# Memory queries and memory outputs on scaled float16 pairs in a hybrid attention block on Trainium2

## The chip, the cores and the metric

The kernel runs on one core of one Trainium2 chip. Its time is the device time of one execution in microseconds (us). Times before and after are medians of a few executions; a profile is one further execution, with every instruction recorded. The engines are named as in the profile: PE multiplies matrices (PEld is its loading of weights), DVE is the vector engine, ACT the scalar engine, POOL is GpSimd, and SP issues nearly all DMAs.

## What is computed

One layer on x (1024 rows of 1024), with a memory of 256 rows; each sub-layer stands between two RMS norms, and its output is added to x. Cut to what matters:

```
def memory_cross_attention(h, mem_n, w_mq, w_mk, w_mv, w_mo):
    q = (h @ w_mq).reshape(B, S, MEM_HEADS, MEM_HEAD_DIM)      # 4 heads of 256
    k = (mem_n @ w_mk).reshape(B, M, MEM_HEADS, MEM_HEAD_DIM)
    v = (mem_n @ w_mv).reshape(B, M, MEM_HEADS, MEM_HEAD_DIM)
    logits = einsum('bshd,bmhd->bhsm', q, k) * (MEM_HEAD_DIM ** -0.5)
    p = softmax(logits)
    o = einsum('bhsm,bmhd->bshd', p, v).reshape(B, S, D_MODEL)
    return o @ w_mo

    h = rmsnorm(x, g_mix_pre);  proj = h @ w_in
    y = [forgetting attention (8 heads), chunked attention (8 heads)], each normed, concatenated
    x = x + rmsnorm(y @ w_out, g_mix_post)
    h = rmsnorm(x, g_mem_pre);  mem_n = rmsnorm(mem, g_mem_kv)
    x = x + rmsnorm(memory_cross_attention(h, mem_n, ...), g_mem_post)
    h = rmsnorm(x, g_ff_pre)
    x = x + rmsnorm(square(relu(h @ w_ff1)) @ w_ff2, g_ff_post)
```

All inputs and the output are float32.

## The kernel before

**Products from pairs.** Every large product is computed from two parts of each operand, a high part (the value rounded to a narrower type) and a low part (what is left), by three matmuls: high by high, high by low, low by high (`mm3`, lines 203 to 206). The parts are fp32r, a four-byte form of float32, or float16. Before the change the q, k and v projections of the attention and the whole MLP use float16 pairs; float16 has a small range of exponents, so there the weights are first brought to a known size by a power of two that is computed from their squares. The memory keys and values, the output projection `w_out`, the memory queries (`mq`) and the memory output (`ym`) use fp32r pairs without scales.

**Stages.** The opening computes the norm of x and the first values, written out by hand in order, up to about 58 us of the profile. Then comes the attention phase: projections of eight pairs of heads, scores, softmax, turning of the probabilities and products with the values, and, as filler, the memory's keys and values. The second phase holds the output projection (`yw`, with matmuls from 511 us), the rows with their norms (`close_row`), the turning of the rows (`tr_h2T`), the queries, the memory attention and its output. The queries of all 1024 rows and the output of the first 512 rows are computed with seven products in place of eight quarter products (a Strassen scheme, `QUERIES` and `PRODUCTS`), for which sums and differences of weight blocks and of operands are made beforehand (`QuerySums`, `Sums`, `Forms`, `operand_parts`). The other 512 rows of the output are plain (`product_steps` and the rows at the end). The MLP follows from about 830 us to the end.

**What sets the order.** Between the opening and the MLP no order is written by hand. The class `Flow` is a planner that runs while the program is built. It keeps a time of its own; a stream of PE steps gives for each step a cost and a condition, and at each point the first stream whose step is ready is taken. Work of the other engines is handed to `flow.put(engine, earliest time, cost, call, what follows, level)`: of the waiting items that could start, the one with the lowest level is emitted next. The engines on the chip then run their own instructions in the order emitted, and semaphores make them wait for data. So a wrong cost in the plan does not make the result wrong, but it puts an instruction in a queue ahead of others that could have run. `flow.free` holds the times at which each engine is free at the start; `BUSY` sets them after the opening (DVE 8.0, ACT 5.0, POOL 5.5). Tiles are counted by tokens in `free`: a step waits until the plan has one.

**The weights.** `Stock` loads each block of 128 x 1024 float32 (line 459), has ACT make the high part (`hi`, line 508; for q, k and v line 498) and DVE, or for some mk blocks POOL in two halves, the low part (`lo`, lines 514 and 518). Three raw tiles are in flight at most. `needs` says which tiles a block takes.

**Lines that the prediction touches.** Line 471 computes the squares of a q, k or v block on ACT, line 481 sums them on PE (`nq`), line 493 scales a block on POOL. Lines 2254 to 2256 are the last conversions of the opening: for each of eight pieces of the second half of x, ACT makes the high part and DVE (POOL for pieces 6 and 7) the low part, emitted one after the other ahead of the planned phase. Line 338 is a cast of value weights on POOL in the opening. Lines 745 to 747 are the softmax scaling on POOL, line 1746 the same in the memory attention. Line 1190 (`square_sum`) is the square of a row on ACT, lines 1422 and 1423 the root of the row's mean square on DVE and POOL, line 1434 the scaled row on ACT. Lines 1226 to 1241 load blocks of `w_mo`, take their differences and store them; lines 1360 to 1374 do so for `w_mq`. Lines 1633 and 1635 split the operands of the queries; line 1741 finds a score row's maximum.

## Time and profile before

| | us |
|---|---|
| median of 3 executions (lowest, highest) | 1422.49 (1420.89, 1424.1) |
| the profiled execution | 1422.69 |
| its span, first to last instruction | 1420.7 |

| stage, us | PE busy | DVE busy | ACT busy | POOL busy |
|---|---|---|---|---|
| 0 to 58, opening | 53.96 | 43.44 | 37.98 | 12.27 |
| 440 to 520, last heads, memory keys and values | 79.74 | 65.25 | 67.00 | 37.64 |
| 520 to 607, output projection, rows | 85.35 | 54.91 | 55.99 | 9.86 |
| 830 to 1421, MLP | 577.17 | 510.77 | 377.41 | 67.76 |

Busy time is the time in which an engine executes at least one instruction. Matmuls overlap: each is shown longer than the distance to the next, so a row of the timeline gives its start, its duration, engine, line, operation, the tile written and the tiles read, and the distance of two starts is what a matmul costs. A row of a group gives the line, engine, operation, names, shapes, count, busy time and mean duration, and after the second bar the idle time of the engine just ahead of it with what ended it. A row of the waits gives who waited for whom, the total, the number of times and the longest. The granted clock of PE is 0.999 over the span.

### The profile page before, as it was taken

The page shows a single profiled execution, that of the slowest core. Times are in us where ns is not written, and L with a number is a line of the kernel's source. Part 1 is how long each engine was busy: PE and PEld are TensorE (multiplying, and loading weights), DVE is VectorE, ACT ScalarE, POOL GpSimd, SP SyncE. Part 2 cuts the span into 40 slices and gives each one's busy share as a digit, 9 for nine tenths or more (in the row PEclk, how much of TensorE's full clock was granted, in tenths as well). Part 3 has the DMA queues.
Part 4 walks back from the last instruction along what each step waited for, and adds up shares of the span by engine and source line. Part 5 has one row for each costly group of instructions (what it writes and reads, how often), then busy time and mean ns, then how long its engine had stood idle before and what let it go on. Part 6 is the DMA issues. An engine that isn't in the chain of part 4 may idle for free.

```text
span 1420.7 us, 22525 instructions
## 1 busy us (share of the span) xinstructions
PE 1394.8 (98%) x7681; PEld 917.3 (65%) x7681; DVE 1152.9 (81%) x1863; ACT 987.1 (69%) x1688; POOL 452.6 (32%) x615
## 2 busy tenths in 40 slices
PE   8999999999999999999999999999999999999998
PEld 8746666666668988787888864444444445666653
DVE  7887787877768865779788878677998887899998
ACT  6667888888778855897466545786677757666654
POOL 2367868887646500221102421003233000000003
PEclk9999999999999999999999999999999999999999
DMA  8132465545526578472234546976888998696885
GB/s 284 49 83 81 130 196 171 170 131 170 146 84 183 176 249 302 171 266 83 75 104 147 193 160 245 338 235 234 290 285 284 362 364 296 233 318 219 313 297 208
DMA packets 118802, 295.72 MB, mean 208 GB/s; under 512 B 13448, under 2 KB 31888, under 8 KB 118688
## 3 DMA queue, kind: packets, MB, share of 16 engines
q1 hardware_dynamic: 118544, 294.03, 61.4%
q8 instruction: 60, 0.98, 0.3%
q14 instruction: 54, 0.44, 0.1%
q10 hardware_dynamic: 144, 0.26, 0.1%
HBM read 220.26 MB, written 65.59 MB: 201 GB/s over the span
## 4 chain that ended last, share of the span: by engine, by line
PE 75%; DVE 10%; ACT 6%; issue 5%; DMA 2%; POOL 1%; SPq 0%; DVEq 0%; ACTq 0%; POOLq 0%
PE ptr L804 4%; PE fx L204 3%; PE fx L206 3%; PE fx L205 3%; PE px L206 2%; PE px L204 2%; PE px L205 2%; PE pv L849 2%; PE yw L204 2%; PE yw L205 2%; PE yw L206 2%; PE mq L205 2%; PE mq L206 2%; PE mq L204 2%; PE k L204 2%
## 5 line engine op out<-in xcount | busy, mean ns | idle before, releaser
L814 ACT ACTIVATE phl<-ptr 128x512 f16<-128x512 f32 (+3 forms) x152 | 79.5, 537 | 25.5 <-PE ptr L804 22.7
L2900 POOL TENSOR_SCALAR rf<-sf 128x1 f32<-128x1 f32 x7 | 5.8, 826 | 280.3 <-ACT jf L2879 280.0
L2595 POOL TENSOR_TENSOR sc<-wf,wf 128x512 f32<-128x512 f32 x8 | 11.2, 1396 | 172.4 <-DMA wf<-in_w_ff 122.8
L810 DVE SCALAR_TENSOR_TENSOR phl<-ptr,phl 128x384 f16<-128x384 f32 (+1 forms) x76 | 45.8, 616 | 14.5 <-ACT phl L814 14.1
L1746 POOL TENSOR_SCALAR mp<-mp,mst 128x256 f32<-128x256 f32 x32 | 21.3, 673 | 108.8 <-DVE mst L1745 102.1
L812 DVE TENSOR_TENSOR phl<-ptr,phl 128x384 fp32r<-128x384 f32 (+1 forms) x76 | 46.6, 617 | 8.5 <-ACT phl L814 7.8
L2744 ACT ACTIVATE vhif<-ra,fsc 128x1024 f16<-128x1024 f32 x34 | 38.9, 1144 | 21.1 <-PE fx L206 10.2
L849 PE MATMUL pv<-phl,vs 128*128 128x512 f32 (+1 forms) x152 | 52.8, 428 | 0.0
L2746 DVE SCALAR_TENSOR_TENSOR vhif<-ra,fsc,vhif 128x1024 f16<-128x1024 f32 x34 | 43.5, 1281 | 10.6 <-ACT vhif L2744 10.3
L2744 ACT ACTIVATE whif<-ra,fsc 128x1024 f16<-128x1024 f32 x34 | 38.9, 1143 | 18.8 <-PE fx L206 10.3
L204 PE MATMUL yw<-whiwo,yT_hi 128*128 128x512 f32 x128 | 50.8, 397 | 0.0
L205 PE MATMUL yw<-wlowo,yT_hi 128*128 128x512 f32 x128 | 50.2, 392 | 0.0
L206 PE MATMUL yw<-whiwo,yT_lo 128*128 128x512 f32 x128 | 50.1, 391 | 0.0
L204 PE MATMUL fx<-vlof,vhif 128*128 128x512 f16 x128 | 48.5, 379 | 0.8 <-DVE yc L2951 0.8
L204 PE MATMUL q<-hF_hi,wq 128*128 128x512 f16 x128 | 48.9, 382 | 0.2 <-DVE qs L953 0.2
L204 PE MATMUL k<-hF_hi,wk 128*128 128x512 f16 x128 | 49.0, 383 | 0.0
L2746 DVE SCALAR_TENSOR_TENSOR whif<-ra,fsc,whif 128x1024 f16<-128x1024 f32 x34 | 43.5, 1280 | 6.5 <-ACT whif L2744 6.4
L206 PE MATMUL q<-hF_hi,wq 128*128 128x512 f16 x128 | 48.5, 379 | 0.0
L204 PE MATMUL fx<-wlof,whif 128*128 128x512 f16 x128 | 48.5, 379 | 0.0
L205 PE MATMUL fx<-wlof,whif 128*128 128x512 f16 x128 | 48.5, 379 | 0.0
L206 PE MATMUL fx<-wlof,whif 128*128 128x512 f16 x128 | 48.5, 379 | 0.0
L205 PE MATMUL k<-hF_lo,wk 128*128 128x512 f16 x128 | 48.5, 379 | 0.0
(855 smaller groups left out, 5338.5 us busy)
## 6 DMA issues: line engine op xcount, KB each, us to landing
wg<-in_w_ff SPq DMA_DIRECT2D x48, 512.0 KB, 5.7
ra<-gd SPq DMA_DIRECT2D x40, 512.0 KB, 5.3
wf<-in_w_ff SPq DMA_DIRECT2D x38, 512.0 KB, 4.8
wn<-in_w_ff SPq DMA_DIRECT2D x32, 512.0 KB, 4.9
w2n<-in_w_ff SPq DMA_DIRECT2D x32, 512.0 KB, 6.0
wi<-in_w_ff2q SPq DMA_DIRECT2D x28, 512.0 KB, 5.5
gd<-s SPq DMA_DIRECT2D x32, 256.0 KB, 5.6
gd<-g SPq DMA_DIRECT2D x19, 256.0 KB, 5.0
```

The lines of the kernel that those rows point to most:

```text
L204: nc.tensor.matmul(ps, lh, rh, start=start, stop=False, skip_group_check=more)
L205: nc.tensor.matmul(ps, lh, rl, start=False, stop=False, skip_group_check=more)
L206: nc.tensor.matmul(ps, ll, rh, start=False, stop=stop, skip_group_check=more)
L804: nc.tensor.transpose(tr[:, m, :], sp[:, k * P:(k + 1) * P], ident)
L810: flow.put("V", at, 0.75, lambda: nc.vector.scalar_tensor_tensor(pl[:, live, :], tr[:, live, :], 2.0 ** 14, ph[:, live, :], op0=ALU.mult, ...
L812: if ph.dtype == F16 else nc.vector.tensor_sub(pl[:, live, :], tr[:, live, :], f(ph[:, live, :])), done)
L814: flow.put("S", flow.end, 0.6, lambda ph=ph, tr=tr, live=live: nc.scalar.activation(ph[:, live, :], tr[:, live, :], AF.Copy, scale=2.0 ** ...
L849: nc.tensor.matmul(pv[:, :, qs_, :], v, hl[:, :, hs, :], start=c == 0 and turn == 0, stop=last)
L1746: mul = lambda st=st, pr=pr: nc.gpsimd.tensor_scalar(pr, pr, st[:, 2:3], 1.0, op0=ALU.mult, op1=ALU.mult)
L2595: eng.tensor_sub(sc[:, k1], r0[:, k0], r1[:, k0])
L2744: nc.scalar.activation(ah, ra, AF.Copy, scale=su)
L2746: nc.vector.scalar_tensor_tensor(al, ra, su, ah, op0=ALU.mult, op1=ALU.subtract)
```

## The change

**Pairs.** The blocks of `w_mq` and `w_mo` and the operands that meet them (the forms of the queries, the operands of the Strassen products, the outputs of the second half) become float16 pairs. One tile holds high and low part, so each takes half as many buffers.

**Scales.** Two numbers per side bring the operands to size. For the queries: the squares of all blocks of `w_mq` (16 new squares on ACT, in `QuerySums`) and of `g_mem_pre` are summed by one small matmul, and from them come powers of two `smq` (weights) and `sgm` (multiplied into `g_mem_pre`), and `uq`, which takes both out again and holds the factor 0.0625. For the output: the squares of all blocks of `w_mo` (16, in `Sums`) and of the memory values (2) give `smo` and `sov`; `sov` goes into the scaling of the memory probabilities on POOL, and `um` (into `g_mem_post`) and `um32` (into the squares) take both out. New streams `query_scale_steps` and `output_scale_steps` hold the two matmuls. The conversion of a `mq` block waits for the query scales, that of a `mo` block and every memory score for the output scales.

**High parts on POOL.** All blocks mk, mv, wo, mq and mo get their high part from POOL in place of ACT. The scaled rows 1, 3, 5 and 7 move from ACT to POOL.

**The opening.** The eight pieces of lines 2254 to 2256 are handed to the planner; `BUSY` becomes DVE 5.6, ACT 4.5, POOL 7.4, and the plan holds the first k weights and the squares of the second q block as done at 5.9 and 0.5.

**Order.** Nearly all levels given to `flow.put` change, some streams change places, the costs in the plan follow the new types (0.681 to 0.655 for three query matmuls, 1.362 to 1.31 for six of the output), some small tiles get more buffers, and the starts and distances of background loads change.

```
+    fsm, mfx = const.tile([P, 42], F32, name="fsm"), const.tile([P, 8], F32, name="mfx")
+    gmem, gmsq = (const.tile([P, KC], F32, name=k) for k in ("gmem", "gmsq"))
...
+            if key[0] in ("mq", "mo"):
+                shape.insert(1, 2)
+                x = (u4(nm, shape, F16) if home == "u4" else
+                     (p2x if home == "wq" else wp).tile(shape, F16, tag=home, bufs=2, name=nm))
+                self.w[key] = x[:, 0], x[:, 1]
+                c = smq if key[0] == "mq" else smo
+                if eng == "G":
+                    return nc.gpsimd.tensor_scalar(x[:, 0], raw, c, 1.0, op0=ALU.mult, op1=ALU.mult)
+                return nc.scalar.activation(x[:, 0], raw, AF.Copy, scale=c)
...
-            nc.scalar.activation(w[0], raw, AF.Copy)
+            if eng == "G":
+                nc.gpsimd.tensor_copy(w[0], raw)
+            else:
+                nc.scalar.activation(w[0], raw, AF.Copy)
...
+            if key[0] in ("mq", "mo"):
+                return eng.scalar_tensor_tensor(lo, raw, smq if key[0] == "mq" else smo, hi, op0=ALU.mult, op1=ALU.subtract)
...
-                if not free[home].ready(n):
+                if not free[home].ready(n) or not there(*{"mq": ("query scales",), "mo": ("output scales",)}.get(key[0], ())):
...
-                flow.put("S", flow.now, 1.06, lambda key=key: self.hi(key), halves, 2)
+                e = {"mk": "G", "mv": "G", "wo": "G", "mq": "G", "mo": "G"}[key[0]]
+                flow.put(e, flow.now, 1.06 if e == "S" else 1.15, lambda key=key, e=e: self.hi(key, e), halves, 3)
...
-        START, PACE = 100.0, 12.0
+        START, PACE = 20.0, 14.0
...
+            landed = all_of(("sum blocks", i, a), 4, lambda at: [flow.put("S", at, 0.65, lambda k=k, c=24 + i * 8 + a * 4 + m: square_sum(
+                r[k], fsm[:, c:c + 1], HT, 1.0), squared, 5) for m, k in enumerate(names4)])
...
-            form_q[n] = [u4(f"{n}q_{m}{i}", (P, 2, HT)) for m in "hl" for i in range(2)]
+            both = [u4(f"{n}q{i}", (P, 2, 2, HT), F16) for i in range(2)]
+            form_q[n] = [both[i][:, m] for m in range(2) for i in range(2)]
...
-                    yield (0.72, lambda: there(("qm", th, h, 0), ("qm", th, h, 1)) and free["s"].ready()
+                    yield (0.72, lambda: there(("qm", th, h, 0), ("qm", th, h, 1), "output scales") and free["s"].ready()
...
-                        pr, pr, st[:, 2:3], 1.0, op0=ALU.mult, op1=ALU.mult)
+                        pr, pr, st[:, 2:3], sov, op0=ALU.mult, op1=ALU.mult)
...
-            opt[n, k] = u4(f"{n}o{k}", (P, 2, 2, Q))
+            opt[n, k] = u4(f"{n}o{k}", (P, 2, 2, Q), F16)
...
-                            outs[th, h] = u4(f"oT_hi{th}{h}", (P, 2, HT)), u4(f"oT_lo{th}{h}", (P, 2, HT))
+                            x = u4(f"oT{th}{h}", (P, 2, 2, HT), F16)
+                            outs[th, h] = x[:, 0], x[:, 1]
...
-        yield 0.87, lambda: flow.now > GATES and free["tr"].ready(2)
+        yield 0.87, lambda: flow.now > GATES and there(*(("hF", kc) for kc in range(KC))) and free["tr"].ready(2)
...
+    def late_half(kc, x):
+        eng = "G" if kc in LATE else "V"
+        hi = lambda: nc.scalar.activation(hF[1].hi(kc), x, AF.Copy)
+        lo = lambda: (nc.gpsimd if eng == "G" else nc.vector).tensor_sub(hF[1].lo(kc), x, hF[1].hi(kc))
+        flow.put("S", 0.0, 0.63, hi, lambda at: flow.put(
+            eng, at, 1.45 if eng == "G" else 1.15, lo, mark(("hF", kc)), 1), 3)
+
-    LATE, RAWS, GATES, BUSY = (6, 7), (0.0, 3.5), 5.0, dict(V=8.0, S=5.0, G=5.5)
+    LATE, RAWS, GATES, BUSY = (6, 7), (0.0, 3.5), 5.0, dict(V=5.6, S=4.5, G=7.4)
...
         for kc in range(KC):
-            x, e = xT[1][kc // 2][:, kc % 2, :], nc.gpsimd if kc in LATE else nc.vector
-            nc.scalar.activation(hF[1].hi(kc), x, AF.Copy)
-            e.tensor_sub(hF[1].lo(kc), x, hF[1].hi(kc))
+            late_half(kc, xT[1][kc // 2][:, kc % 2, :])
+        seen["k", 0], seen["sq", ("q", 1)] = 5.9, 0.5
...
+        for m in range(2):
+            flow.put("S", 0.0, 1.25, lambda m=m: square_sum(f(vmh[m]), fsm[:, 40 + m:41 + m], D, 1.0), mark(("vm squares", m)), 0)
...
-        flow.run([memory_out_steps(), memory_turn_steps(), memory_score_steps(), rstd_steps(1), second_rows(),
-                  norm_steps(), tail], lambda: stock.to_load or stock.to_split)
+        flow.run([memory_turn_steps(), rstd_steps(1), memory_score_steps(), memory_out_steps(), second_rows(),
+                  norm_steps(), output_scale_steps(), tail], lambda: stock.to_load or stock.to_split)
```

More of the change, by code (lines that the diff above doesn't have):

```diff
@@ L565, in pump @@
                 if key[0] in "qkv":
[L566 removed]
+                    flow.put("S", flow.now, 1.25, lambda key=key: self.squares(key), mark(("sq", key)), 5)
                     continue
@@ L867, in both @@
                             o2[own], pv[own, :, ::step], uv[own], o2[own], op0=ALU.mult, op1=ALU.add), lambda end: (
-                            free["pv"].give(end), store(end)))
+                            free["pv"].give(end), store(end)), 1)
                     flow.put("S", flow.end, 0.45, lambda: nc.scalar.activation(
-                        o2[own], pv[oth, :, ::step], AF.Copy, scale=uv[oth]), both)
+                        o2[own], pv[oth, :, ::step], AF.Copy, scale=uv[oth]), both, 3)
                     return
@@ L966, in then @@
                         flow.put("V", at, 0.75, lo, lambda end: (last(end), flow.load(
-                            end, lambda: copy(l), part, 3.6)), 1)
-                    flow.put("S", flow.end, 0.7, hi, then, 1)
+                            end, lambda: copy(l), part, 3.6)), 5)
+                    flow.put("S", flow.end, 0.7, hi, then, 2)
         if 1 in halves:
@@ L1272, in squares @@
                     nc.vector.tensor_reduce(wsq[:, n:n + 1], r[0], axis=mybir.AxisListType.X, op=ALU.max)
-            flow.load(flow.now, load, lambda at: flow.put("S", at, 1.25, squares, lambda end: (free["u4"].give(end), seen.__setitem__(("wn", n), end)), 5))
+            flow.load(flow.now, load, lambda at: flow.put("S", at, 1.25, squares, lambda end: (free["u4"].give(end), seen.__setitem__(("wn", n), end)), 3))
     def rsqrt(x, k):
@@ L1350, in pump @@
                 _, call, then = self.parts.pop(0)
-                flow.put("V", flow.now, 0.7, call, then, 5)
+                flow.put("V", flow.now, 0.7, call, then, 2)
                 self.at = flow.now + self.PACE
@@ L1355, in unit, with squares @@
             r = {}
-            landed = all_of(("query sums", nb), 4)
+            squared = all_of(("query sums", nb), 4)
+            def squares(at):
+                for m, k in enumerate(("B11", "B12", "B22", "B21")):
+                    flow.put("S", at, 0.65, lambda k=k, c=nb * 4 + m: nc.scalar.activation(
+                        self.junk, r[k], AF.Square, accum_out=fsm[:, c:c + 1]), squared, 5)
+            landed = all_of(("query blocks", nb), 4, squares)
             for k, (kh, nh) in {"B11": (0, 0), "B12": (0, 1), "B22": (1, 1), "B21": (1, 0)}.items():
@@ L1443, in wait @@
             else:
-                flow.put("G", end + 0.5, 0.0, lambda: None, wait)
-        flow.put("G", at, 1.9, lambda: root(0, ss[:, 0:1], ss[:, 1:2]), wait, 0)
+                flow.put("G", end + 0.5, 0.0, lambda: None, wait, 1)
+        flow.put("G", at, 1.9, lambda: root(0, ss[:, 0:1], ss[:, 1:2]), wait, 5)
     def mix_steps(g):
@@ L1697, in query_steps @@
             if i:
-                for _ in range(4):
+                for _ in range(2):
                     free["u4"].give(flow.end)
```

217 lines of the change are left out of this document (130 added, 87 removed).

## The prediction

> **What bounds the kernel now.** I read the page first, then the busy time by stages, then the waits of PE, and last single rows of the timeline.
>
> ```profile
> span 1420.7 us, 22525 instructions
> ...
> PE 1394.8 (98%) x7681; PEld 917.3 (65%) x7681; DVE 1152.9 (81%) x1863; ACT 987.1 (69%) x1688; POOL 452.6 (32%) x615
> ```
>
> The page gives PE busy in 1394.8 of 1420.7 us, so PE is idle for 25.9 us in all. The profiled execution took 1422.69 us; 2.0 us of it lie around the span. The median of the three runs, 1422.49, is 0.2 us lower, and I shift the sum by that at its end.
>
> With PE at 98%, only two things make the program shorter: matmuls that follow each other faster, or less idle PE. The stages (columns: us, then PE, PEld, DVE, ACT and POOL busy) show where the change could do either:
>
> ```profile
> 58.00:100.00 42.00, 37.73 (x184) 17.15 (x182) 34.58 (x50) 31.01 (x50) 27.70 (x28) 1.00 0.32 91
> 100.00:440.00 340.00, 339.63 (x2006) 227.77 (x2005) 258.76 (x617) 274.90 (x556) 244.64 (x387) 1.00 0.48 144
> ...
> 607.00:830.00 223.00, 221.21 (x1121) 185.04 (x1120) 185.22 (x303) 142.85 (x277) 52.69 (x66) 1.00 0.44 145
> ```
>
> From 58 to 100 us, where the opening's conversions run, PE is idle for 42.00 - 37.73 = 4.3 us; in the attention stage that follows for 0.4 us. From 607 to 830 us, which holds the memory queries, attention and output, it is idle for 1.8 us, and DVE is busy in 185 of 223 us, ACT in 143. There the pace of the matmuls sets the end, with DVE next. What ended PE's idle time, first in the opening (window 0 to 100), then around the memory stage (511 to 830):
>
> ```profile
> PE nq L481 <- ACT wk L471: 2.6, 2, 2.1
> ```
>
> ```profile
> PE tr_h2T L1555 <- ACT yw L1434: 1.6, 1, 1.6
> PE mq L205 <- DVE A12q_l L1635: 0.7, 1, 0.7
> PE mq L205 <- DVE A22q_l L1635: 0.6, 1, 0.6
> ```
>
> **Float16 pairs.** These rows of the tiles mq and ym give the counts:
>
> ```profile
> 0.00:1421.00 1421.00, 82.34 (x336) 1.00 0.62 208
> ```
>
> ```profile
> L204 PE MATMUL ym<-whimo,oT_hi x64: 389/389/476, 779.3 to 829.1; 128*128 128x512 f32 x64
> ...
> L204 PE MATMUL ym<-whimo_B,A11o x8: 389/396/437, 715.8 to 723.6; 128*128 128x512 f32 x8
> ```
>
> The queries are 336 matmuls. The outputs of the second half are three passes (L204 to L206) of 64, 192; those of the first half are seven products of three passes of 8, 168. That is 696 matmuls of 512 columns, all fp32r now, all float16 after. Durations overlap, so I take the distance between starts. First and last of 13 consecutive query matmuls, then of 18 output matmuls, then of 22 float16 ones in the first MLP product:
>
> ```profile
> 663.07 0.39 PE L206 MATMUL mq<-S2q_h,wlomq_T 128*128 128x512 f32 x1
> ...
> 665.79 0.39 PE L206 MATMUL mq<-S2q_h,wlomq_T 128*128 128x512 f32 x1
> ```
>
> ```profile
> 720.08 0.39 PE L204 MATMUL ym<-whimo_B,A11o 128*128 128x512 f32 x1
> ...
> 724.01 0.39 PE L206 MATMUL ym<-whimo_B,A11o 128*128 128x512 f32 x1
> ```
>
> ```profile
> 836.92 0.38 PE L205 MATMUL px<-h3T_lo,whi_a 128*128 128x512 f16 x1
> ...
> 841.45 0.38 PE L205 MATMUL py<-h3T_lo,whi_a 128*128 128x512 f16 x1
> ```
>
> 2.72 / 12 = 226.7 ns, 3.93 / 17 = 231.2 ns, 4.53 / 21 = 215.7 ns. The gain is 11.0 to 15.5 ns each; I take the middle, 13.2, since both fp32r rows are from this stage: 696 x 13.2 ns = 9.2 us, with bounds of 7.7 and 10.8. It lies on PE, which sets the end there, if DVE lets it.
>
> [...]
>
> **The high parts that go to GpSimd.** All conversions of the 60 weight blocks mk, mv, wo, mq and mo (line 508) leave ACT, and GpSimd gets them. The columns are ACT's busy time and count; then the nearest rows of GpSimd, a scaling of 1024 columns and a cast of 512:
>
> ```profile
> 0.00:1421.00 1421.00, 62.87 (x60) 1.00 0.62 208
> ```
>
> ```profile
> L493 POOL TENSOR_SCALAR wrawk<-wrawk,wsc 128x1024 f32<-128x1024 f32 x8 | 9.0, 1119 | 0.8 <-ACT wk L524 0.8
> ```
>
> ```profile
> L338 POOL CAST whiv<-wrawv 128x512 fp32r<-128x512 f32 x4 | 3.4, 868 | 9.1 <-DMA wrawv<-in_w_v 9.1
> ```
>
> Between 60 x 1.12 = 67 us and 60 x 2 x 0.87 = 104 us enter a GpSimd that is busy for 452.6 us in all and 52.7 of the 223 us. I take 1.12, the row with the right number of columns. The 36 query and output blocks (14, 14 and 8) put 40 us there: room enough. Behind a conversion in GpSimd's queue stand the softmax scalings (L1746, L747) and the row roots (L1423); PE's 1.6 us wait on ACT's yw is behind such a root. Ahead of ACT's rows stands a microsecond less for each block, and four of the eight row scalings of L1434 leave ACT too. The three waits around the memory stage sum to 2.9 us; the two on DVE stay, part of the first goes: a gain of 1.0, bounds +2 (roots later) and -2.9.
>
> The low part after such a conversion is computed by DVE from two SBUF operands. Three rows of DVE, 1024 columns each: the scaled form that the query and output blocks get now, the plain form in the memory stage, and the plain form of mk, most of which runs while GpSimd is busy for 16.5 of 20 us (GpSimd's time is the last of the five in the second fence):
>
> ```profile
> L2746 DVE SCALAR_TENSOR_TENSOR whif<-ra,fsc,whif 128x1024 f16<-128x1024 f32 x34 | 43.5, 1280 | 6.5 <-ACT whif L2744 6.4
> ...
> L514 DVE TENSOR_TENSOR wlomq_T<-wrawmq_T,whimq_T 128x1024 fp32r<-128x1024 f32 x8 | 9.7, 1218 | 0.0
> ...
> L514 DVE TENSOR_TENSOR wlomk<-wrawmk,whimk 128x1024 fp32r<-128x1024 f32 x4 | 5.9, 1487 | 0.7 <-ACT whimk L508 0.7
> ```
>
> ```profile
> 440.00:460.00 20.00, 19.74 (x163) 18.71 (x162) 17.12 (x37) 18.11 (x38) 16.53 (x21) 1.00 0.56 167
> ```
>
> The scaled form adds 62 ns x 36 = 2.2 us to DVE. A collision adds 269 ns; if each of the 36 conversions meets one, 9.7 us. With about 3 us of small scale arithmetic (some 15 operations of at most 0.2 us), DVE has 185.2 + 2.2 + 9.7 + 3 = 200 us of work in a stage of 223 - 9.2 = 214 us: not the bound, but with little to spare in its fullest stretches. I price it at a loss of 1.0, bounds 0 and 4.
>
> [...]
>
> **The scales.** 16 squares of query blocks and 16 of output blocks join ACT, and two of 1024 columns:
>
> ```profile
> L1190 ACT ACTIVATE junk<-yw 128x512 bf16<-128x512 f32 x16 | 10.1, 630 | 6.1 <-DVE yw L1474 5.9
> ```
>
> 32 x 0.63 and two of at most twice that are 23 us, most of them at the lowest rank of ACT's list, against the 62.87 us that leave it. Two small matmuls on PE cost at most one full step each, 2 x 0.23 = 0.5; I take 0.4, bounds 0 and 1. The new waits: no query block is converted before the query scales, no memory score starts before the output scales. In before the last difference block of the output weights is issued at 557.5 and the first score starts at 625.4:
>
> ```profile
> L1241 SPq DMA_DIRECT2D T4d<-B21r x4: 319/320/320, 528.6 to 557.5; - x4
> ```
>
> ```profile
> L204 PE MATMUL ms<-km_hi,qh x64: 277/280/370, 625.4 to 778.6; 128*128 128x256 f32 x64
> ```
>
> With 10 us allowed for landing, 10 us for 16 squares and 5 us for the root and its arithmetic (estimates; the squares from the row above), the scales are there near 583, some 40 us ahead of the score. What is queued behind that wait is the whole memory attention, but the wait ends first. The query sums start 80 us earlier than before, so theirs ends earlier still. Both at 0.
>
> **The opening.** Eight high and eight low parts go from a fixed place into the list, with the engines' real busy times as its start. In before they sit in one block, and the square that PE waits for stands behind the eight:
>
> ```profile
> 62.47 4.28 ACT L2255 ACTIVATE hF_hi<-xT 128x512 f16<-128x512 f32 x8
> ...
> 67.84 0.38 PE L481 MATMUL nq<-nq,o 128*128 128x1 f32 x2 [2.13 <-ACT wk L471]
> ```
>
> The norm matmul waits 2.13 us in PE's in-order queue with projections behind it that could run. A list that knows of the 4.28 us puts it later: a gain of 2.1. What is late next is DVE's or GpSimd's share of the first heads; bounds from all the idle of this stretch, -4.3, to a loss of 1. The changed ranks and the order of the streams elsewhere move no work: 0, with 2 either way, since PE is full from 100 to 440 us.
>
> **Sum.** -9.2 - 1.0 + 1.0 + 0.4 - 2.1 = -10.9: 1422.7 - 10.9 = 1411.8 for a profiled execution, 1411.6 as a median.
>
> **Rivals.** (1) DVE becomes the bound of the memory stage and the kernel is slower. If each of the 36 conversions held DVE for its whole 1.12 us, DVE would have 185.2 + 40.3 + 5.2 = 230.7 us of work in a stage that now takes 223: 7.7 longer, less the opening's 2.1, 1428.3. The gain shrinks from (214 - 190.4) / 36 = 0.65 us a conversion, where DVE fills the stage, and is gone at about 0.95. The 0.27 speaks against it, DVE's 83% for it. (2) The float16 matmuls follow no faster: 1411.8 + 9.2 = 1421.0, no change that can be told. The three spacings speak against it. (3) GpSimd is late with the mk and mv blocks, whose low halves and softmax scalings it does already: 16 blocks at 1.74 rather than 1.12 us are 10 us more, of which perhaps half reaches PE: 1417. (4) All idle time of the opening and the three waits go, and the spacing saves its upper figure: 1422.7 - 10.8 - 4.3 - 2.9 + 0.4 = 1405.1.
>
> **Chances.** Forecast 0.64, (1) 0.07, (2) 0.06, (3) 0.15, (4) 0.08. The terms' bounds carry the forecast's own case from about 1407 to 1416; with (3) and (4) the range is 1405 to 1418. 0.2%, about what a measurement of this kernel can tell, is 2.8 us: faster ends at 1419.6. Faster 0.87, same 0.07, slower 0.06.
>
> **What would show it.** Right: the mq and ym starts 215 to 217 ns apart, the wait of nq on ACT gone, 60 conversions on GpSimd at about 1.1 us, DVE under 95% from 607 to the end of ym. Wrong: PE waiting for low parts of mq or mo on DVE, the low parts well over 1.5 us, PE waiting on mk or mv, the first score waiting for the output scales, or a longer stretch before 607 us.

## The result and the profile after

The changed kernel takes 1454.3 us (median of 4 executions, 1451.84 to 1456.02) against 1423.05 us before (4 executions): the ratio is 1.022, with a 95% interval of 1.020 to 1.024. It is slower by 31 us where 11 us less were forecast. One execution of a kernel below, the one with the old levels for the attention alone, took 2417.19 us at a mean granted clock of 0.555, against 0.985 to 0.993 in its other three, and is left out of that kernel's figures.

The page of the changed kernel, its span and the busy times of its engines:

```profile
span 1453.2 us, 22621 instructions
...
PE 1403.6 (97%) x7685; PEld 864.7 (60%) x7685; DVE 1170.8 (81%) x1881; ACT 953.5 (66%) x1694; POOL 556.8 (38%) x682
```

The span is 32.5 us longer. PE is idle for 49.6 us (25.9 before), which is 23.7 of them. PE is also busy for 8.8 us more, although its matmuls were to follow each other faster. So two things need an explanation: new holes, and matmuls that became slower somewhere.

The same stages as in the prediction, with bounds moved to where the work now lies: opening, attention, memory. The columns are again us, PE, PEld, DVE, ACT and POOL busy, then the granted clock of PE.

```profile
58.00:100.00 42.00, 41.18 (x202) 19.94 (x201) 35.91 (x54) 34.44 (x64) 25.29 (x28) 1.00 0.40 116
100.00:460.00 360.00, 346.43 (x2004) 231.48 (x2003) 259.97 (x626) 282.20 (x580) 259.26 (x397) 0.98 0.43 133
...
630.00:863.00 233.00, 218.77 (x1122) 125.83 (x1122) 197.50 (x302) 113.26 (x240) 116.30 (x103) 0.97 0.42 140
```

The opening is better: 0.8 us of idle PE where before had 4.3. The attention takes 20 us more, with 13.6 us idle against 0.4 in before's 340 us. The memory stage has 14.2 us idle against 1.8. And in these two the clock is 0.98 and 0.97, where each of before's stages shows 1.00.

**The first loss: attention.** What ACT and then PE waited for from 100 to 440 us in the changed kernel (total, times, longest):

```profile
ACT o L897 <- DMA od<-o: 10.6, 3, 6.3
ACT o L897 <- POOL o L894: 8.0, 2, 6.1
```

```profile
PE vtr L1002 <- DVE phl L829: 5.5, 2, 4.6
PE pv L868 <- ACT phl L831: 4.0, 1, 4.0
```

Line 897 copies one half of a group's attention output out of PSUM into a small tile, `o2`; DVE adds the other half, POOL adds the two halves of the tile (L894), and a DMA stores it, after which its buffer is free. Before, where the line has the number 880, ACT waited there once:

```profile
ACT o L880 <- DMA od<-o: 0.8, 1, 0.8
```

One of these waits in the timeline, first POOL, then the issue of the stores, then ACT, then PE (start, duration, engine, line, tiles; in brackets the idle time ahead of it and what ended it):

```profile
283.54 1.16 POOL L495 TENSOR_SCALAR wrawq<-wrawq,wsc 128x1024 f32<-128x1024 f32 x1 [0.23 <-DVE wsc L490]
284.68 1.54 POOL L495 TENSOR_SCALAR wrawv<-wrawv,wsc 128x1024 f32<-128x1024 f32 x1
286.20 1.12 POOL L495 TENSOR_SCALAR wrawk<-wrawk,wsc 128x1024 f32<-128x1024 f32 x1
287.28 0.29 POOL L709 TENSOR_SCALAR_AFFINE_SELECT biasf<-biasf 128x128 f32<-128x128 f32 x1
287.54 0.71 POOL L894 TENSOR_TENSOR o<-o 64x256 f32<-64x256 f32 x1
...
289.52 0.72 POOL L894 TENSOR_TENSOR o<-o 64x256 f32<-64x256 f32 x1
```

```profile
288.28 2.44 SPq L877 DMA_DIRECT2D od<-o  x2
```

```profile
290.31 0.59 ACT L897 ACTIVATE o<-pv 64x512 f32<-64x512 f32 x1 [6.06 <-POOL o L894]
290.93 0.60 ACT L831 ACTIVATE phl<-ptr 128x512 fp32r<-128x512 f32 x1
```

```profile
287.17 0.60 PE L821 MATMUL ptr<-ident,spf3g 128*128 128x128 f32 x4
292.39 1.09 PE L1002 MATMUL vtr<-ident,vt 128*128 128x128 f32 x4 [4.62 <-DVE phl L829]
...
294.14 0.65 PE L204 MATMUL v<-hF_hi,wv 128*128 128x512 f16 x1
294.58 0.63 PE L205 MATMUL v<-hF_lo,wv 128*128 128x512 f16 x1
```

Read it from the last row back. PE stands for 4.62 us because the probabilities (`phl`) are late. ACT, which writes their high part (L831), has that instruction queued right behind an `o2` copy, and the copy stands for 6.06 us. It needs the buffer of the copy two before it, whose POOL add starts only at 287.54 and whose store is issued at 288.28 and lands 1.9 us later, at 290.20. (The row names POOL because the second add, on the other buffer, ends at 290.24.) The first add stands behind three weight scalings of 1.1 to 1.5 us. The change made the levels so: the scalings went from 2 to 0, the add from 0 to 1, and the copy stays at 0, and the lower level goes first. The planner never learns that the copy cannot start, since it does not count the two buffers of `o2`.

The hole is not all. After it the matmuls take 0.63 to 0.65 us where they take 0.38, and three windows of 20 us show the clock:

```profile
280.00:300.00 20.00, 15.38 (x76) 9.27 (x75) 9.89 (x22) 10.99 (x21) 12.28 (x19) 0.83 0.20 64
320.00:340.00 20.00, 15.61 (x82) 9.75 (x81) 8.85 (x20) 13.05 (x28) 10.31 (x19) 0.83 0.48 146
620.00:640.00 20.00, 13.76 (x62) 9.32 (x61) 19.07 (x23) 15.91 (x31) 12.79 (x10) 0.87 0.98 337
```

**The second loss: memory.** Here PE waits in several places, above all in `PE mtr L1849 <- POOL mp L1827` with 4.0 us in three waits, and in one wait each in `mq L204 <- ACT A11q L1714` with 3.2, `mq L205 <- DVE A11q L1716` with 3.0 and `ym L204 <- DVE h3T_lo L1605` with 2.6. No single one of them makes up the loss, so most of the experiments are about this stage.

### The profile page after: what moved, and what is told of

It reads as the page before. It is cut to its first block, busy times and chain, and to the rows that moved or that the text cites. A ratio compares the mean times of both kernels' runs of the same rounds, so it can differ in the third digit from the quotient of the medians.

```text
span 1453.2 us, 22621 instructions
## 1 busy us (share of the span) xinstructions
PE 1403.6 (97%) x7685; PEld 864.7 (60%) x7685; DVE 1170.8 (81%) x1881; ACT 953.5 (66%) x1694; POOL 556.8 (38%) x682
## 4 chain that ended last, share of the span: by engine, by line
PE 38%; DVE 9%; issue 4%; POOL 4%; ACT 4%; DMA 2%; SPq 0%; DVEq 0%; ACTq 0%; POOLq 0%
PE fx L204 3%; PE fx L206 3%; PE fx L205 3%; PE px L206 1%; PE px L205 1%; PE px L204 1%; PE ym L204 1%; PE ym L206 1%; PE ym L205 1%; PE fi L204 1%; PE fi L206 1%; PE fi L205 1%; PE mq L205 1%; PE mq L204 1%; PE mq L206 1%
## 5 line engine op out<-in xcount | busy, mean ns | idle before, releaser
L831 ACT ACTIVATE phl<-ptr 128x512 f16<-128x512 f32 (+3 forms) x152 | 80.7, 537 | 37.9 <-PE ptr L821 36.3
L204 PE MATMUL yw<-whiwo,yT_hi 128*128 128x512 f32 x128 | 50.8, 397 | 1.7 <-ACT yw L1549 0.9
L205 PE MATMUL yw<-wlowo,yT_hi 128*128 128x512 f32 x128 | 49.9, 390 | 0.0
L204 PE MATMUL k<-hF_hi,wk 128*128 128x512 f16 x128 | 49.7, 388 | 0.0
L204 PE MATMUL q<-hF_hi,wq 128*128 128x512 f16 x128 | 49.1, 384 | 0.2 <-DVE qs L970 0.2
L204 PE MATMUL fx<-vlof,vhif 128*128 128x512 f16 x128 | 48.5, 379 | 0.8 <-DVE yc L3043 0.8
L205 PE MATMUL k<-hF_lo,wk 128*128 128x512 f16 x128 | 49.1, 384 | 0.0
L206 PE MATMUL k<-hF_hi,wk 128*128 128x512 f16 x128 | 49.0, 383 | 0.0
L205 PE MATMUL q<-hF_lo,wq 128*128 128x512 f16 x128 | 48.8, 381 | 0.0
L204 PE MATMUL fx<-wlof,whif 128*128 128x512 f16 x128 | 48.5, 379 | 0.0
L205 PE MATMUL fx<-wlof,whif 128*128 128x512 f16 x128 | 48.5, 379 | 0.0
```

What stands on the lines that cost most here:

```text
L204: nc.tensor.matmul(ps, lh, rh, start=start, stop=False, skip_group_check=more)
L205: nc.tensor.matmul(ps, lh, rl, start=False, stop=False, skip_group_check=more)
L206: nc.tensor.matmul(ps, ll, rh, start=False, stop=stop, skip_group_check=more)
L831: flow.put("S", flow.end, 0.6, lambda ph=ph, tr=tr, live=live: nc.scalar.activation(ph[:, live, :], tr[:, live, :], AF.Copy, scale=2.0 ** ...
```

## The experiments

Three theories stood at the start. Theory 1: the new levels put instructions at the head of in-order queues, where they wait for a buffer (`o2`) that the list does not count. Theory 2: the conversions on POOL block DVE's work, or POOL's own. Theory 3: the squares, sums and scales crowd ACT and the DMA queue. Theory 4 was added after the first four runs: any new order costs by itself, since the old one happens to have few holes.

### Levels, buffers and engines of the changed kernel

**Old levels, all of them.** The changed kernel with before's levels, stream order, room counts and load starts, and with all scaled rows on ACT; pairs, scales, POOL's high parts and the opening stay.

```
-                        flow.put(eng, at, 1.28 if key[0] in ("mq", "mo") else 1.22, lambda: self.lo(key, e), last, 3)
+                        flow.put(eng, at, 1.28 if key[0] in ("mq", "mo") else 1.22, lambda: self.lo(key, e), last, 1)
...
-                    o2[own], pv[oth, :, :, ::step], AF.Copy, scale=1.0), both, 0)
+                    o2[own], pv[oth, :, :, ::step], AF.Copy, scale=1.0), both)
```

> The kernel after with every rank, stream order, start time and pace of the scheduler's list as in before, and all row scalings on ScalarE; the float16 pairs, the scales, the conversions on GpSimd and the opening's list entries stay. Theory 1 (the new ranks and starts put instructions at the head of in-order queues that wait for a buffer the list does not track, o2 above all): the holes of 4.62 and 4.03 us at 288 and 321 us go with most of the others, and the time falls to what the prediction's terms give, 1411 to 1418. Theory 2 (GpSimd's conversions block): 1440 or more, with the same waits. Theory 3 (the squares, sums and scales that float16 needs crowd ScalarE and the DMA queue): 1435 or more.

1445.91 us, ratio 1.0162 (1.0147 to 1.0177): 8 us of the 31 come back. The old levels do not bring the old order back, since other instructions are now ranked by them.

**Old levels for the attention alone.** The changed kernel with the old levels, stream order and load starts where they act ahead of the memory stage, such as these; the memory stage keeps its new ones.

```
-        START, PACE = 20.0, 14.0
+        START, PACE = 100.0, 12.0
...
-                flow.put("V", flow.now, 0.7, call, then, 2)
+                flow.put("V", flow.now, 0.7, call, then, 5)
```

> Only the ranks, orders and starts that act before the memory stage (attention, weight conversions, early sums) as in before; those of the memory stage stay as in after. Theory 1: the about 20 us lost between 100 and 460 us come back, 1430 to 1436, and the holes from 629 us on (3.25, 2.99, 2.21, 2.60) stay. Theories 2 and 3: under 8 us back, 1446 or more.

1466.82 us (three executions, 1460.49 to 1469.83), 1.0301 (1.0268 to 1.0335): slower than the change itself. Half the old levels and half the new ones make yet another order, and a worse one.

**Four o2 buffers.** The same order in every queue as in the changed kernel, instruction for instruction.

```
-                o2 = p1.tile([P, 2, P] if n > 3 else [P, 2, 2, P], F32, tag="o2", bufs=2, name=f"o2{nm}")
+                o2 = p1.tile([P, 2, P] if n > 3 else [P, 2, 2, P], F32, tag="o2", bufs=4, name=f"o2{nm}")
```

> The kernel after with four o2 buffers in place of two, the order of every queue unchanged. Theory 1 in its narrow form (the two long holes are ScalarE standing at an o2 buffer still held by a GpSimd add or a store): ScalarE's 18.6 us of waits on line 897 go to under 2, both holes go with the lowered clock behind each (0.83 in both 20 us windows), and 12 to 16 us come back: 1438 to 1442. If o2 only hides the next late step (the phl parts or SyncE's stores): under 5 us back, 1449 or more. Theory 2: no change.

1432.96 us, 1.0074 (1.0057 to 1.0091): 21.3 of the 31.2 us are gone with two buffers more, and ACT's waits of line 897 on stores and adds are gone with them. Its busy times by stage, for the same attention and memory work as above:

```profile
100.00:440.00 340.00, 336.81 (x1990) 227.01 (x1989) 258.66 (x625) 282.01 (x580) 257.77 (x396) 1.00 0.46 139
...
608.00:842.00 234.00, 217.93 (x1125) 125.70 (x1125) 197.19 (x302) 114.61 (x243) 117.15 (x104) 0.97 0.42 141
```

The attention has its 340 us back, at a clock of 1.00. Its page has PE busy for 1391.9 us of a span of 1429.8, so against the changed kernel 11.7 us less idle and 11.7 us less busy. The waits cost as much again in slow matmuls. Theory 1 holds for two thirds of the loss. The memory stage is as bad as it was, at 234 us.

**All high parts on ACT, planned anew.**

```
-                e = {"mk": "G", "mv": "G", "wo": "G", "mq": "G", "mo": "G"}[key[0]]
+                e = dict.fromkeys(("mk", "mv", "wo", "mq", "mo"), "S")[key[0]]
```

> The kernel after with the high parts of all 60 weight blocks on ScalarE again, everything else as after (the list replans with it). Theory 2: the time falls by 15 us or more, below 1440. Theory 1: the part up to 400 us is unchanged, since no converted block is due there; the waits of the memory transposes on GpSimd (4.0 us) go and others come on ScalarE: 1445 to 1460.

1478.87 us, 1.0395 (1.0375 to 1.0415). It says nothing of POOL by itself: the planner places everything anew, and in the new plan PE stands for 7.0 us at `tr_h2T L1635 <- POOL yw L1513` and for 6.8 in two waits at `yw L204 <- ACT yw L1549`.

### Is a new order enough by itself?

**Two nudges of before.** Before's kernel with one planned cost changed, by 1.9% and by 1.3%. The instructions are before's; only their order may change.

```
-                yield (0.648, lambda: kc or there((what, n)) and free["mm"].ready() and
+                yield (0.66, lambda: kc or there((what, n)) and free["mm"].ready() and
```

> The kernel before with one number of the scheduler's list changed, the estimated cost of a projection step, 0.648 to 0.66; no instruction is added, removed or resized, but the order of all queues is planned anew. Theory 4 (what is lost is the price of any new order, which the old one had been spared by its choice of ranks, not the price of a given part of the change): 8 to 30 us slower than before, with new holes of 2 us and more and half clock behind them. Theories 2 and 3 (GpSimd's conversions, the work for the scales): within 3 us of before.

```
-                yield ((0.347 if dead else 0.454) if n < 4 else (0.33 if dead else 0.436), lambda: there(("t", n, a, g, c), ("v", n, 0), ("v", n, 1))
+                yield ((0.347 if dead else 0.46) if n < 4 else (0.33 if dead else 0.436), lambda: there(("t", n, a, g, c), ("v", n, 0), ("v", n, 1))
```

> The kernel before with another number of the list changed, the estimated cost of a value step, 0.454 to 0.46. Theory 4: slower by 5 to 30 us, with holes at other places than those of the other altered number. Theories 2 and 3: within 3 us of before.

1442.36 us (1.0135, 1.0120 to 1.0150) and 1438.53 us (1.0109, 1.0094 to 1.0124): 19 and 15 us for a plan that differs in nothing but order. The waits of PE in the first, from 100 to 850 us:

```profile
PE mtr L1768 <- POOL mp L1746: 5.9, 2, 4.1
PE mq L204 <- ACT S2q_h L1633: 2.6, 1, 2.6
PE mq L204 <- ACT A11q_h L1633: 1.6, 1, 1.6
```

These are the same places as in the changed kernel: the first query operand, the memory probabilities. Theory 4 holds as a sufficient cause for a loss of 15 to 19 us. Both nudges that were tried are slower; two are too few to say that any new order would be.

**Old levels and old engines.** The old-levels kernel with all high parts on ACT and four `o2` buffers, planned anew.

```
-                e = {"mk": "G", "mv": "G", "wo": "G", "mq": "G", "mo": "G"}[key[0]]
+                e = dict.fromkeys(("mk", "mv", "wo", "mq", "mo"), "S")[key[0]]
```

> Float16 pairs, scales and the opening's list entries with the ranks, orders, starts and row scalings of before, all high parts on ScalarE and four o2 buffers. If the parts cost what the prediction said and only the moved ones hurt: 1411 to 1416. Theory 4: 1420 to 1445, with the attention stage free of o2 waits and holes elsewhere. Theory 3: holes behind squares and sums of the scales.

1452.77 us, 1.0210 (1.0193 to 1.0227). This kernel does not return the layer's output, and the record does not show why. So its time is no evidence of what the pairs alone would take, and nothing below rests on it.

**Memory blocks on ACT, in place.** The four-buffer kernel; each `mq` and `mo` conversion and each row scaling is planned as on POOL, but issued to ACT at that place.

```
-                flow.put(e, flow.now, 1.06 if e == "S" else 1.15, lambda key=key, e=e: self.hi(key, e), halves, 3)
+                flow.put(e, flow.now, 1.06 if e == "S" else 1.15, lambda key=key, e=e: self.hi(key, "S" if key[0] in ("mq", "mo") else e), halves, 3)
```

> After with four o2 buffers, and the high parts of the query and output blocks and the four row scalings computed by ScalarE at the places that the list had planned on GpSimd; DVE's and SyncE's orders are unchanged. Theory 2 for the memory stage (GpSimd takes up to 3 us for a 1.1 us operation while DVE reads two operands): the waits of the memory transposes on GpSimd (4.0 us) and of the first query product (5.5 us and its half clock) shrink, 8 to 14 us back: 1419 to 1425. If ScalarE's and DVE's order sets these holes: within 4 us of 1433, either side.

1429.76 us, 1.0051 (1.0036 to 1.0066): 3.2 us less than with POOL. That is POOL's price for these blocks and rows in this order, hardly clear of the noise, since the two intervals overlap; 6.6 us above before are left. Two effects partly cancel: PE's wait `mtr L1849 <- POOL mp L1827` falls from 4.0 to 1.6 us, and the one on `A11q` of ACT (L1714), which now has more to do, grows from 3.2 to 5.3.

### Each part in before's own order

To take the planner out of it, these kernels keep before's order of all its instructions; the new work is entered beside it at no planned cost.

**Pairs in the old order.** Float16 pairs and scales in before; high parts on ACT, two `o2` buffers, old opening. The squares of the query blocks stand where the loads are planned to land.

```
-            nc.scalar.activation(w[0], raw, AF.Copy)
+            nc.scalar.activation(w[0], raw, AF.Copy, scale=(smq if key[0] == "mq" else smo) if pairs else 1.0)
...
-            landed = all_of(("query sums", nb), 4)
+            landed = all_of(("query sums", nb), 4, squares)
```

> The float16 pairs and their scales alone, with the order of before: the list keeps its old costs, ranks and streams, and the added squares, two small matmuls and scale arithmetic enter at no cost in the list, so that no other instruction changes its place in any queue. High parts on ScalarE, two o2 buffers, the old opening. Theory 4 (the parts cost about what was predicted, the new order costs the rest): 1412 to 1417, that is 1423.1 - 9.2 + 0.4 with up to 3 us given back where conversions don't keep up with the faster matmuls. Theory 3 (the work for the scales): 1425 or more.

1441.36 us, 1.0127 (1.0113 to 1.0141). ACT's rows in the attention stage, then what PE does next:

```profile
168.41 0.63 ACT L1426 ACTIVATE sqj<-B11q 128x512 bf16<-128x512 f32 x1 [0.84 <-DMA B11q<-in_w_mq]
...
172.31 0.63 ACT L1426 ACTIVATE sqj<-B21q 128x512 bf16<-128x512 f32 x1 [1.19 <-DMA B21q<-in_w_mq]
```

```profile
174.65 1.01 PE L855 MATMUL pv<-phl,vs 128*128 128x512 f32 x2 [2.93 <-DVE phl L818]
```

A planned landing is early by a microsecond, four squares stand in ACT's queue and wait for DMAs, and PE stands for 2.93 us behind them. The two small matmuls, `mon` and `mqn`, stand ahead of their data too: PE waits 1.7 and 1.5 us at them (L1354).

**High parts on POOL in the old order.** Before with one line changed: the 60 conversions go to POOL at the places that they had on ACT.

```
-            nc.scalar.activation(w[0], raw, AF.Copy)
+            nc.gpsimd.tensor_copy(w[0], raw)
```

> Before with one thing changed: the high parts of the 60 weight blocks of mk, mv, wo, mq and mo are computed by GpSimd at the places of the list where ScalarE had them. Theory 4: within 4 us of before. Theory 2 (GpSimd's conversions block): 1432 or more, with PE waiting for GpSimd's softmax scalings or DVE's low parts.

1439.43 us, 1.0115 (1.0101 to 1.0129): 17 us slower. Its conversions by block (shortest, median and longest in ns, first and last start), four of the eight rows:

```profile
L508 POOL CAST whimk<-wrawmk x8: 1033/1042/2045, 380.7 to 465.6; 128x1024 fp32r<-128x1024 f32 x8
L508 POOL CAST whimv<-wrawmv x8: 1037/1042/2180, 471.6 to 500.5; 128x1024 fp32r<-128x1024 f32 x8
...
L508 POOL CAST whimo<-wrawmo x8: 1035/1265/2039, 775.7 to 823.5; 128x1024 fp32r<-128x1024 f32 x8
L508 POOL CAST whimq_B<-wrawmq_B x6: 1035/1449/1742, 600.0 to 686.9; 128x1024 fp32r<-128x1024 f32 x6
```

and the busy times of its stages, against before's 70.74 of 71 and 221.21 of 223 us:

```profile
440.00:511.00 71.00, 66.56 (x480) 58.75 (x480) 58.34 (x117) 43.67 (x98) 53.96 (x60) 1.00 0.52 166
...
608.00:831.00 223.00, 215.05 (x1082) 177.68 (x1081) 189.44 (x300) 112.41 (x247) 93.36 (x92) 1.00 0.40 136
```

A conversion of mk or mv takes 1.04 us on POOL in the median, where it took 1.05 on ACT in before, but single ones take up to 2.18. PE is idle for 4.4 us in the first stage and 8.0 in the memory stage, the longest wait being 2.6 us for `A12q_l`, a low part of DVE. The 60 conversions take 73.9 us together, where 60 at 1.04 us would take 62. Theory 2 holds in this order. How much of it is the longer conversions and low parts (up to 2.29 us, 1.76 in before), and how much a POOL queue that the plan had left no room in, was not separated.

**Both.**

```
+            if pairs:
+                nc.gpsimd.tensor_scalar(w[0], raw, smq if key[0] == "mq" else smo, 1.0, op0=ALU.mult, op1=ALU.mult)
+            else:
+                nc.gpsimd.tensor_copy(w[0], raw)
```

> Both: the float16 pairs and the high parts on GpSimd, in the order of before. Theory 4: the sum of the two differences within 3 us, 1410 to 1420. Theory 2: 1425 or more although the pairs alone gain.

1456.18 us, 1.0236 (1.0222 to 1.0250). The two losses, 18.8 and 16.9 us, add to 35.7; 33.6 were measured. So they hardly overlap.

### The scales

**Constant scales in the old order.** The pairs in the old order, with constants for the scales: squares, sums and the two small matmuls are left out.

```
+    for k, x in enumerate((128.0, 4.0, 128.0, 8.0, 0.0625 / 512.0, 1.0 / 1024.0, 1.0 / 32768.0)):
+        nc.vector.memset(mfx[:, k:k + 1], x)
```

> The float16 pairs in the order of before with nothing measured for the scales: the powers of two are written as constants (this part of the computation is left out), so that the squares, sums and the two small matmuls are gone; 8 small memsets and the two products with the scales stay. If the pairs are worth what the prediction said: 1412 to 1418, all of it after 631 us of the kernel before's memory stage, and the 18.8 us that the measured scales cost with this order (in the run of the pairs alone) is the squares standing in ScalarE's queue for their blocks. If the pairs themselves lose (their conversions or the GpSimd products with a second scale): 1424 or more.

1418.81 us, 0.9968 (0.9956 to 0.9979): the only kernel below before, and 22.6 us below the one with measured scales. This is the cleanest look at the float16 matmuls. Its memory stage, and the first and last of the three passes of one product:

```profile
608.00:825.00 217.00, 212.57 (x1124) 125.00 (x1124) 186.76 (x303) 147.63 (x277) 58.56 (x67) 1.00 0.45 148
```

```profile
L204 PE MATMUL mq<-S1q_h,whimq_T x16: 379/379/379, 670.1 to 679.8; 128*128 128x512 f16 x16
...
L206 PE MATMUL mq<-S1q_h,wlomq_T x16: 379/379/379, 670.5 to 680.2; 128*128 128x512 f16 x16
```

48 matmuls start from 670.1 to 680.2, so 10.1 / 47 = 215 ns apart. The stage takes 217 us where before took 223, with PE busy for 8.6 us less.

**No scale work in the changed kernel's order.** The four-buffer kernel with constants; squares, sums and the scales' arithmetic are left out, each at its place; the two small matmuls stay.

```
-            landed = all_of(("sum blocks", i, a), 4, lambda at: [flow.put("S", at, 0.65, lambda k=k, c=24 + i * 8 + a * 4 + m: square_sum(
-                r[k], fsm[:, c:c + 1], HT, 1.0), squared, 5) for m, k in enumerate(names4)])
+            landed = all_of(("sum blocks", i, a), 4, lambda at: [flow.put("S", at, 0.65, lambda: None, squared, 5) for m, k in enumerate(names4)])
```

> After with four o2 buffers and the scales as constants: the squares, sums and scale arithmetic are taken out where they stood (this part of the computation is left out), and every other instruction keeps its place. Theory 3 for the memory stage: 8 us or more back from 1433, below 1425. If the order sets the holes there: within 4 us of 1433.

1433.36 us, 1.0067 (1.0051 to 1.0082), against 1432.96 with the scales: nothing.

**The same, with the memory blocks on ACT.** The edit is that of the run above with the memory blocks on ACT.

```
-                flow.put(e, flow.now, 1.06 if e == "S" else 1.15, lambda key=key, e=e: self.hi(key, e), halves, 3)
+                flow.put(e, flow.now, 1.06 if e == "S" else 1.15, lambda key=key, e=e: self.hi(key, "S" if key[0] in ("mq", "mo") else e), halves, 3)
```

> The same without scale work (this part of the computation is left out), and with the high parts of the query and output blocks and the four row scalings on ScalarE at their places. What is then left above 1423 - 9.2 - 4 = 1410 is neither GpSimd's conversions in the memory stage nor the work for the scales, but the places themselves: expected 1424 to 1430 by theory 4; 1412 to 1418 if theories 2 and 3 together make up the loss of the memory stage.

1430.28 us, 1.0050 (1.0037 to 1.0064), against 1429.76: nothing again. Where the squares have a place in the plan, theory 3 falls; it holds only where they are put ahead of their data.

**Measured scales, squares placed late.** The pairs in the old order with measured scales; each square stands just ahead of the DVE subtraction that overwrites its block, and the small matmuls follow 10 us after.

```
                     square(place)
...
+        yield 0.0, lambda: there("gmsq") and flow.now > seen["gmsq"] + 10.0 and free["tr"].ready(2)
```

> Pairs with measured scales, every other instruction in the order of before; each square now stands just ahead of the subtraction that overwrites its block or some microseconds before it, not four in a row where the block is expected to land, and each small matmul is issued 10 us after its squares. If the 22.6 us between the pairs with measured and with constant scales were squares that waited in ScalarE's queue for blocks not yet landed, and PE waiting for them: most come back, 1419 to 1428. If it is the squares' own 0.65 us on ScalarE: 1432 or more.

1425.01 us over 12 executions, 1.0012 (1.0003 to 1.0021): 16.4 of the 22.6 us are back, and the kernel is within 0.2% of before. The 6.2 us that are left above the constant scales were not taken apart.

**The same with the output squares in the plan.** The sums wait for the squares, so the planner moves things from 511 us on.

```
+                    flow.put("S", at + 1.5 + 0.8 * m, 0.0, lambda k=k, c=24 + i * 8 + a * 4 + m: square_sum(r[k], fsm[:, c:c + 1], HT, 1.0), squared, 9)
+            squared = all_of(("sums squared", i, a), 4, lambda at: flow.chain(at + 1.0, parts_, stores, 2))
```

> The same, but for the output weights the squares have the lowest rank and the sums come after them, so that the list plans the stage from 511 us anew. Theory 4 (a new order costs by itself): 8 us or more slower than the one that keeps the order, up to 1445. If only the squares' places count: equal to it within 3 us.

1433.58 us, 1.0085 (1.0073 to 1.0097): 8.6 us for the new order after 511 us.

## Why the prediction was wrong

The step that failed is the last sentence of the opening's part: "The changed ranks and the order of the streams elsewhere move no work: 0, with 2 either way, since PE is full from 100 to 440 us." A PE that is full shows that the old order has no holes. It says nothing of the next order, and it leaves no slack in which a hole could hide. At one buffer of this order 21.3 us are lost (four `o2` buffers, shown), and a change of one planned cost by 1.3%, which moves nothing but order, already makes 15 (shown). Nor was it the levels alone: with the old ones back, 23 us are still lost. The sum had no term at all for the new plan that every other edit brings with it.

Point by point, by the prediction's own terms:

- **Float16 pairs, -9.2: the pace right, the gain at the end half of it.** Starts are 215 ns apart. In before's order PE is busy for 8.6 us less in the memory stage. Only part reaches the end even there: 0.32%, 4.6 us (interval 3.0 to 6.3), since PE then waits 2.3 us for the first MLP weights (`px L204 <- ACT whi_a L2370`), which came only 0.3 us late before, and 1.6 us for the memory probabilities. Rival 2 falls.
- **High parts on POOL, -1.0 (+2 to -2.9): wrong in sign and outside its bounds.** In before's order they cost 16.9 us, in the changed order the 36 memory blocks and four rows 3.2. The duration was right in the main, with medians of 1.04 to 1.41 us for the blocks. What was missing is the spread, 1.03 to 2.99 us: the prediction counted POOL's free time and took one duration for each. Rival 3 falls: the mk and mv blocks take 1.04 us in the median, and no wait of PE in the changed kernel is put down to them.
- **Collisions on DVE, +1.0 (0 to 4): the stage right, the price of one too low, their number too high.** DVE is busy for 197.5 of 233 us, so it is not the bound, and rival 1 falls. But a low part took up to 0.9 us longer, not 0.27, and never the 1.12 of rival 1: the row of the `mq_B` low parts, the worst of the five blocks (shortest, median and longest in ns), shows 1.26 us at the least and 2.14 at most. Only 7 of the 36 low parts take more than 1.35 us, each beside a POOL instruction of 1024 columns; of the other 29, 20 overlap work of POOL as well and take 1.26 to 1.29. All 36 lose 4.9 us together, where the prediction allowed for 9.7. How much of POOL's price comes this way and how much through POOL's own late ends was not separated.

```profile
L528 DVE SCALAR_TENSOR_TENSOR mq_B<-wrawmq_B,mfx,mq_B x6: 1260/1890/2135, 617.6 to 690.0; 128x1024 f16<-128x1024 f32 x6
```

- **Scales and waits for them, 0 and 0: right** in the changed order, where leaving the work out gives nothing and no wait of PE on the scales shows. The +0.4 of the small matmuls no run there tested. In the other order it was 22.6 us, so it was the place, not the work, that made it free. One cost of the scales the sum did not have: the scaling of the memory probabilities on POOL now reads a second number from a tile. In before's order with constant scales its median goes from 479 to 556 ns, and PE waits 1.6 us for the result, where before shows no such wait; in the changed kernel, with the conversions in the same queue, it is 740 ns and 4.0 us. First before, then the changed kernel (shortest, median, longest in ns):

```profile
L1746 POOL TENSOR_SCALAR mp<-mp,mst x32: 470/479/1822, 628.5 to 784.3; 128x256 f32<-128x256 f32 x32
```

```profile
L1827 POOL TENSOR_SCALAR mp<-mp,mst,mfx x32: 547/740/2493, 659.0 to 802.6; 128x256 f32<-128x256 f32 x32
```

- **Opening, -2.1 (-4.3 to +1): right, at its lower bound.** The wait of `nq` is gone, and idle PE from 0 to 100 us falls from 8.3 to 4.1 us. No run has this part alone.
- **Levels and order, 0 (2 either way): wrong,** as above.

The balance goes by profiled spans, with the four-buffer kernel as the step between. From it to the changed kernel are 23.4 us, half waits and half slow matmuls. From before to it are 9.1 us. Its idle PE grew by 12.0: 14.3 in the memory stage (16.1 against 1.8) and 2.8 in the attention (3.2 against 0.4), less 4.1 in the opening and 1.0 in the rest. Its busy PE fell by 2.9, where the pairs give some 8.6 to 9.2 and the memory stage's clock of 0.97 takes an estimated 0.03 x 218 = 6.5 back. So the memory stage alone loses some 20 us to holes and their aftermath.

**What stays open** is which places of the new order make those 20 us. The share of POOL's 36 blocks and four rows is some 3 us, and that of the squares, sums and arithmetic of the scales is 0. The four-buffer kernel's own waits name the places, but not a single reason:

```profile
PE ym L204 <- DVE h3T_lo L1605: 4.4, 1, 4.4
PE mtr L1849 <- POOL mp L1827: 4.0, 3, 2.2
PE mq L204 <- ACT A11q L1714: 3.2, 1, 3.2
PE mq L205 <- DVE A11q L1716: 2.3, 1, 2.3
```

For the first of them the timeline gives a likely reason, which no run tested: ACT waits 5.1 and 3.1 us for the loads of two MLP weights, with the squares queued behind them that free PSUM for the output rows.

No version with measured scales beat before. Pairs in the old order with late squares come within 0.2% of it, and constants would give 0.3%.

## What to carry to other kernels

In a kernel whose queues are written by a planner, an edit is priced as its own work plus a new plan, and on a full engine the second can be many times the first (PE is busy for 98% of before's span, and the two nudges, which have no work of their own, cost 19 and 15 us): before believing a gain, change one cost by 1 to 2% and see what any new order costs. Test a part with all other instructions in their old places. And look in the new order for instructions that wait for something that the planner does not count (a buffer, a load's true landing), because everything behind it in the queue waits too: here a copy that stood for 6.06 us on ACT became 4.62 us of idle PE.

## What the runs showed of the hardware

**One hole in PE of 2.1 us cost nearly as much again, another nothing.** In before, PE waits 2.13 us for `wk` at 65.7 us and goes on at full pace, its matmuls 215 ns apart. In the second nudge the same hole of the same length comes 0.1 us earlier, and this follows:

```profile
67.72 0.38 PE L481 MATMUL nq<-nq,o 128*128 128x1 f32 x2 [2.12 <-ACT wk L471]
67.96 0.58 PE L204 MATMUL k<-hF_hi,wk 128*128 128x512 f16 x1
68.34 0.63 PE L205 MATMUL k<-hF_lo,wk 128*128 128x512 f16 x1
68.76 0.63 PE L206 MATMUL k<-hF_hi,wk 128*128 128x512 f16 x1
...
71.32 0.43 PE L206 MATMUL k<-hF_hi,wk 128*128 128x512 f16 x1
```

From 67.96 to 71.32 us the matmuls take up to 0.63 us, at 0.43 us from start to start, which is half the pace, and then it is over: 8 steps in 3.36 us, where at 215 ns they would take 1.7. The clock of the window shows it too; first before, then the nudge:

```profile
68.00:72.00 4.00, 3.43 (x20) 1.59 (x21) 3.90 (x7) 1.04 (x2) 2.78 (x7) 1.00 0.06 20
```

```profile
68.00:72.00 4.00, 4.00 (x14) 1.57 (x15) 3.87 (x6) 0.91 (x2) 2.65 (x7) 0.57 0.05 15
```

Around the 4.62 us hole of the changed kernel the spell is twice as long: the granted clock from 290 to 297 us is 0.51. In the clock records of the changed kernel's trace seven spells at 0.5, the kernel's last 3 us aside, start at 174.1, 290.1, 324.3, 467.6, 634.9, 805.5 and 839.7 us; each lasts 3.41 or 6.83 us, and any two starts lie a whole multiple of 3.41 us apart, wherever the holes lie. In before the same records show 1.0 up to the last 2 us. So a hole of 2.12 us was followed by such a spell, and one of 2.13 us was not; why, no run shows.

**On POOL one conversion of 1024 columns took from 1.1 to 3.0 us.** In the changed kernel, the shortest, median and longest of the query conversions:

```profile
L509 POOL TENSOR_SCALAR mq_T<-wrawmq_T,mfx x8: 1109/1171/2849, 634.2 to 701.6; 128x1024 f16<-128x1024 f32 x8
...
L509 POOL TENSOR_SCALAR mq_B<-wrawmq_B,mfx x6: 1132/1414/2992, 616.1 to 687.0; 128x1024 f16<-128x1024 f32 x6
```

The longest conversion is 1.9 us above the shortest, more than one whole DVE low part of 1.3 us. While the one of 2.85 us stood, from 634.17 us, DVE ran a low part of `A11q` of 1.21 us from start to end and began the next, which took 2.05 us; beside the one of 2.99 us, from 686.98 us, it ran one of `S2q` of 1.22 us. So both conversions and the second low part of `A11q` took longer than the shortest of their rows; that one held up the other is not shown.
